# First modulation quarter copied by ScalarE and turned in another PSUM tag; at the end, last squares summed by TensorE and two products on GpSimd

## The chip, the cores and the metric

The kernel runs on one core of one Trainium2 chip. The metric is the device time of one execution in microseconds (us), from the start of the program to its end. The core's engines work in parallel, each through a list of instructions in its own fixed order, and wait for one another through semaphores: TensorE (PE; its weight loads are shown as PEld), VectorE (DVE), ScalarE (ACT), GpSimd (POOL) and SyncE (SP), which here only issues DMA transfers.

## The reference

The program is the trunk of a diffusion model: two layers over 512 latent and 256 context tokens, model width 1024, batch 1, in fp32, and a final RMSNorm of the latent tokens. Each layer scales and shifts its normalised input by a modulation vector that is computed from the conditioning vector (adaLN), runs two mixers in parallel on it, adds their output, and then runs an MLP with a hidden width of 4096:

```python
def rmsnorm(x, w):
    y = xf * lax.rsqrt(jnp.mean(xf * xf, axis=-1, keepdims=True) + NORM_EPS)
    return (y * w.astype(F32)).astype(x.dtype)
def modulate(h, shift, scale):
    return h * (1.0 + scale) + shift
def sq_relu_mlp(h, w1, w2):
    return jnp.square(jax.nn.relu(h @ w1)) @ w2
```

Layer 0 has global attention beside a bidirectional RWKV-7 scan, whose state carries from token to token: S_t = S_{t-1} (diag(w_t) - kk_t^T (a_t * kk_t)) + v_t^T k_t, y_t = S_t r_t. Layer 1 has windowed attention beside a bidirectional Mamba-2 mixer. The output is the latent stream after the last RMSNorm.

## The kernel before

Activations lie with the model width on the 128 partitions (eight tiles, k = 0 to 7) and tokens along the free axis. Every large product is made of three passes in fp32r: each operand is split in a rounded part and a remainder (`split`, L279 on ACT and L280 on DVE, tiles whi/wlo for weights, hh/hl or dh/dl for activations), and PE adds whi·hh, whi·hl and wlo·hh in PSUM (`product`, L367; the rows are named after what they make: win, wout, m). Weights come from memory in 512 KB pieces through SP into tiles wraw (and wmod for the modulation's), a few ahead.

The code says what depends on what; the order in which each engine's instructions stand is set by a scheduler that plays the whole program through with simulated times (`schedule_with_timeline_sim=True`) and takes what is ready, with parts of the code marked as urgent (`tc.high_priority()`). So an edit in one place can move instructions far from it. Tiles come from pools with a number of buffers; PSUM tiles go by tags ("s", "mod", "w"), and a tile waits until the one before it in its tag is free.

Three places matter.

*The head.* The first product of layer 0 (`win`) needs the modulation of layer 0 and the norm of x. `first_modulation(q)` makes one of four quarters: 4 times 16 matmuls (L428) into PSUM tile mod, a copy into SBUF (mrows, L431), a turn by PE (modt, L433), and an addition of the bias on DVE (modT, L435). For quarter q the tiles k = 2q and 2q+1 of the normed input follow: nscale (L452), ny (L497), hh (L498), hl (L500). The norm is made by squares (nsq, L470), their sums over k (acc, L471), `rms_rows`: sums over partitions by PE against ones (nsum, L479), a power -1/2 on DVE and POOL (nr, L381, L382), split (nrs), a diagonal (ndiag, L486), and a broadcast by PE (nbc, L490); ACT copies it for later use (rb, L550).

*Scan and attention of layer 0.* The scan goes through the tokens in steps (rows s, x, xs, u, vu, y, yacc by name) and leaves PE waiting between steps; the attention's matmuls (scores sc, turned probabilities pt, values po) fill in. The results go through memory (oD) and come back as the operand of the output product: `raw<-oD` (L1293), split into xr and dh/dl, then `wout` (L1302). yt turns the scan's output, gg are gates that are loaded for it (L1087, L1088), oy is the gated output.

*The tail.* The MLP of layer 1 does its last products (m, eight tiles) first for the first half of the latent tokens, LATS[0], then for the second, LATS[1]. Each tile is added to xl (`update`, L1223) and squared (`add_squares`; the last addition is on DVE). `to_out` scales xl by the norm's weight (L1768), calls `rms_rows`, and multiplies pairs of tiles by the broadcast row (L1778), and SP sends them out (L1779). For the first half the row is first copied to SBUF (rms, L1773). In the product the variable `eng` is set and not used:

```python
                eng = G if s == LATS[0] and k < 4 else V
                V.tensor_tensor(out=xs, in0=xs, in1=bc.unsqueeze(1).to_broadcast([P, 2, s[1]]), op=ALU.mult)
```

Of the kernel before, what the change touches and what calls it, by code (L numbers as in the profile page):

```python
# [18 lines left out]
P = 128  # L19
D = 1024  # L20
KT = 8
# [203 lines left out]
def tile_trunk(ctx: ExitStack, tc: tile.TileContext, t: dict, out, cc: Cols, pc: Cols):  # L225
# [69 lines left out]
    def at(t, s):  # L295

        if s == OUTER:
            return t[:, NCTX:NT].rearrange("p (b c) -> p b c", c=P)[:, ::3]
        return t[:, s[0]:s[0] + s[1]]
# [50 lines left out]
    def row(x, k, s):  # L350
        return x.at(k, s) if isinstance(x, Stream) else at(x[:, k], s)
# [67 lines left out]
    def first_modulation(q, np_):  # L419

        ps = psum("mod", "mod")
        for kp in range(KT // 2):
            wm = np_.tile([P, 1024], F32, tag="wm", name=u("wmod"), bufs=6)
            nc.sync.dma_start(wm, t["wmod0"][q, kp])
            for j in range(2):
                k = 2 * kp + j
                for r in range(4):
                    T.matmul(ps[32 * r:32 * r + 32, 0:P], lhsT=cs[:, k, :], rhs=wm[:, 512 * j + P * r:512 * j + P * r + P],  # L428
                             start=k == 0, stop=k == KT - 1, tile_position=(0, 32 * r))
        rows = np_.tile([P, P], F32, tag="mrows", name=u("mrows"), bufs=2)  # L430
        V.tensor_copy(out=rows, in_=ps[:, 0:P])  # L431
        pt = psum("s", "modt")
        T.transpose(pt[:, 0:P], rows, ident)  # L433
        ks = slice(2 * q, 2 * q + 2)
        V.tensor_tensor(out=modT[:, 0, 0:16, :].rearrange("p (s k) v -> p s k v", s=2)[:, :, ks],  # L435
                        in0=pt[:, 0:P].rearrange("p (s k r) -> p s k r", s=2, k=2)[:, :, :, 0:2],
                        in1=Q("bmod", 0, 16).rearrange("p (s k) -> p s k", s=2)[:, :, ks].unsqueeze(3).to_broadcast([P, 2, 2, 2]),
                        op=ALU.add)
# [22 lines left out]
    onesr = cp.tile([P, P], F32R, name="onesr")  # L461
    V.tensor_copy(out=onesr, in_=ones)

    def add_squares(np_, acc, x, k, s, eng=G):

        if k == 0:
            A.activation(out=at(acc, s), in_=row(x, k, s), func=AF.Square)
            return
        sq = np_.tile([P, NT], F32, tag="nsq", name=u("nsq"), bufs=2)
        A.activation(out=at(sq, s), in_=row(x, k, s), func=AF.Square)  # L470
        (V if k == KT - 1 else eng).tensor_tensor(out=at(acc, s), in0=at(acc, s), in1=at(sq, s), op=ALU.add)  # L471

    def rms_rows(np_, acc, s, tag):

        n = s[1] // P
        pr = psum(tag, "nsum")
        for i in range(n):
            c = s[0] + (P if s != OUTER else NLAT - P) * i
            T.matmul(pr[:, 2 * i:2 * i + 2], lhsT=acc[:, c:c + P], rhs=ones[:, 0:2], start=True, stop=True)  # L479
        r = np_.tile([P, 4], F32, tag="nr", name=u("nr"))[:, 0:n]  # L480
        rsqrt(r, pr[:, 0:2 * n:2], 1.0 / D, EPS, n)
        rr = [np_.tile([P, 4], F32R, tag=f"nr{j}", name=u("nrs"))[:, 0:n] for j in (0, 1)]
        split(rr[0], rr[1], r)
        dg = np_.tile([P, 2, n, P], F32R, tag=f"ndiag{n}", name=u("ndiag"))
        for j in (0, 1):
            V.tensor_tensor(out=dg[:, j], in0=ident.unsqueeze(1).to_broadcast([P, n, P]),  # L486
                            in1=rr[j].bitcast(F32).unsqueeze(2).to_broadcast([P, n, P]), op=ALU.mult)
        bc = psum(tag, "nbc")[:, 0:n * P]
        for j in (0, 1):
            T.matmul(bc, lhsT=onesr, rhs=dg[:, j], start=j == 0, stop=j == 1)  # L490
        return bc
# [733 lines left out]
    def mlp(mp, md, l, x, acc, segs, hh, hl, first, parts, then, side=iter(())):  # L1225
# [4 lines left out]
        for g in range(MLPG):  # L1230
# [14 lines left out]
            for n, part in enumerate(parts if last else (segs,)):  # L1245
                for q in range(4):
                    w = weight(t["w2"][l, g, q])
                    if g:
                        advance(side)
                    for i in range(2):  # L1250
                        m = 2 * q + i
                        ps = psum("w", "m2")
                        product([(ps, w, 512 * i)], dh, dl, range(4), (part,))
                        with tc.high_priority() if last and n == len(parts) - 1 else ExitStack():
                            update(l, 5, x, ps, m, part)
                            for s in part if last else ():
                                add_squares(mp, acc, x, m, s, V if n == len(parts) - 1 else G)
                with tc.high_priority() if last and n == len(parts) - 1 else ExitStack():
                    for s in part if last else ():
                        then(s)  # L1260
# [485 lines left out]
    with ExitStack() as se:  # L1746
# [18 lines left out]
        def to_out(s):  # L1765
# [9 lines left out]
            for k in range(0, KT, 2):  # L1775
                xs = xl[:, k:k + 2, ts]
                eng = G if s == LATS[0] and k < 4 else V
                V.tensor_tensor(out=xs, in0=xs, in1=bc.unsqueeze(1).to_broadcast([P, 2, s[1]]), op=ALU.mult)  # L1778
                nc.sync.dma_start(out[:, k:k + 2, ts], xs)  # L1779

        mlp(mp, md, 1, x, acc, LAT, hh, hl, LATS, [(s,) for s in LATS], to_out)
# [22 lines left out]
```

## Time and profile before

| | |
|---|---|
| time, three runs | 2007.57, 2012.63, 2013.88 us (median 2012.63) |
| profiled execution | 2009.51 us, its span 2007.7 us |
| mean granted clock of PE | 0.975 of full speed |
| busy | PE 94%, PEld 77%, DVE 61%, ACT 42%, POOL 15% of the span |
| DMA | 228.18 MB, 113 GB/s over the span |

The profile is of one execution. The span goes from its first instruction to its last. The chain is followed back from the last instruction to whatever released each one; its shares say which engine the end hung on. A row of a group gives the line, engine and operation, output and inputs with their shapes, how often, then busy time in all and the mean in ns of one, then the idle time just before and who ended it.

### The profile page before, as it was taken

How to read it: one execution, taken by the hardware profiler on the slowest of the kernel's cores; microseconds unless marked ns; L12 is line 12 of the kernel's file. 1: busy time of each engine (PE TensorE's matmuls, PEld its weight loads, DVE VectorE, ACT ScalarE, POOL GpSimd, SP SyncE). 2: the span in 40 equal slices, each digit the busy share in tenths (PEclk: the TensorE clock that was granted, in tenths of full speed). 3: DMA queues.
4: the chain of work that ended last, by engine and by line, in shares of the span. 5: the costliest groups of instructions: out<-in, count | busy, mean ns of one | idle time of the engine just before them, and what ended most of it. 6: DMA issues, size and time to landing. Idle time of an engine off the chain costs nothing.

```text
span 2007.7 us, 34218 instructions
## 1 busy us (share of the span) xinstructions
PE 1896.6 (94%) x13992; PEld 1545.1 (77%) x13992; DVE 1215.2 (61%) x2150; ACT 840.7 (42%) x1419; POOL 294.2 (15%) x291
## 2 busy tenths in 40 slices
PE   6999988899998999999999999899899789999997
PEld 4776756776765998888888889778578488888886
DVE  5567979775677765654544444865687464444445
ACT  3344442555544552232223224544566454333335
POOL 0000014432321520000000002310153120000001
PEclk9999998899998999999999999999999799999998
DMA  9355575742414733344444422212101133333333
GB/s 336 121 166 171 182 228 148 156 89 56 98 44 132 251 107 99 122 124 136 125 125 121 136 84 80 76 53 74 32 1 53 32 95 105 95 92 97 95 97 113
DMA packets 147884, 228.18 MB, mean 114 GB/s; under 512 B 65024, under 2 KB 102288, under 8 KB 147600
## 3 DMA queue, kind: packets, MB, share of 16 engines
q1 hardware_dynamic: 140912, 213.54, 36.1%
q10 hardware_dynamic: 5456, 7.73, 1.1%
q0 software_dynamic: 1360, 4.73, 0.7%
q8 instruction: 110, 1.80, 0.4%
q14 instruction: 46, 0.38, 0.1%
HBM read 200.00 MB, written 25.96 MB: 113 GB/s over the span
## 4 chain that ended last, share of the span: by engine, by line
PE 77%; DVE 9%; DMA 7%; ACT 3%; issue 3%; POOL 1%; SPq 0%; DVEq 0%; POOLq 0%; ACTq 0%
PE m L367 37%; PE win L367 13%; PE po L341 4%; DMA wmod<-in_wmod_dram 4%; PE pt L332 3%; PE z L985 2%; DVE wlo L280 2%; PE sc L1147 2%; PE wout L1718 1%; PE wout L1302 1%; PE s L1051 1%; PE mod L405 1%; PE lora L653 1%; PE z L1560 1%; DVE junk L1319 1%
## 5 line engine op out<-in xcount | busy, mean ns | idle before, releaser
L279 ACT ACTIVATE whi<-wraw 128x1024 fp32r<-128x1024 f32 x214 | 226.4, 1059 | 678.0 <-PE m L367 561.0
L280 DVE TENSOR_TENSOR wlo<-wraw,whi 128x1024 fp32r<-128x1024 f32 x214 | 264.4, 1236 | 212.2 <-ACT whi L279 209.4
L367 PE MATMUL m<-hh,whi 128*128 128x512 f32 (+1 forms) x816 | 239.3, 344 | 4.9 <-ACT relu L1241 2.4
L367 PE MATMUL m<-hl,whi 128*128 128x512 f32 (+1 forms) x816 | 241.2, 343 | 0.2 <-POOL hl L503 0.2
L367 PE MATMUL m<-hh,wlo 128*128 128x512 f32 (+1 forms) x816 | 241.3, 344 | 0.0
L367 PE MATMUL m<-dl,whi 128*128 128x256 f32 (+1 forms) x832 | 240.7, 341 | 0.0
L367 PE MATMUL m<-dh,whi 128*128 128x256 f32 (+1 forms) x832 | 238.6, 342 | 1.7 <-DVE xl L1223 1.6
L367 PE MATMUL m<-dh,wlo 128*128 128x256 f32 (+1 forms) x832 | 239.8, 341 | 0.1
L367 PEld LDWEIGHTS m<-dh,whi 128*128 128x128 f32 x832 | 153.3, 188 | 23.9 <-DVE xl L1223 4.9
L367 PEld LDWEIGHTS m<-hh,whi 128*128 128x128 f32 x816 | 152.1, 188 | 24.7 <-ACT relu L1241 2.8
L471 POOL TENSOR_TENSOR acc<-acc,nsq 128x256 f32<-128x256 f32 x42 | 42.8, 1027 | 865.8 <-ACT nsq L470 861.0
L367 PEld LDWEIGHTS m<-hl,whi 128*128 128x128 f32 x816 | 153.6, 188 | 19.4 <-POOL hl L503 0.4
L367 PEld LDWEIGHTS m<-dl,whi 128*128 128x128 f32 x832 | 153.8, 188 | 19.0
L367 PEld LDWEIGHTS m<-dh,wlo 128*128 128x128 f32 x832 | 153.7, 188 | 18.9 <-DVE wlo L280 0.3
L367 PEld LDWEIGHTS m<-hh,wlo 128*128 128x128 f32 x816 | 153.4, 188 | 19.0 <-DVE wlo L280 0.3
L367 PE MATMUL win<-hl,whi 128*128 128x512 f32 (+1 forms) x512 | 162.3, 348 | 4.7 <-POOL hl L503 3.5
L367 PE MATMUL win<-hh,whi 128*128 128x512 f32 (+1 forms) x512 | 162.3, 362 | 2.7 <-ACT hh L498 2.7
L367 PE MATMUL win<-hh,wlo 128*128 128x512 f32 (+1 forms) x512 | 160.2, 345 | 0.0
L1319 DVE SCALAR_TENSOR_TENSOR junk<-wmod,crow 128x1024 f32<-128x1024 f32 x64 | 78.5, 1226 | 118.5 <-DMA wmod<-in_wmod_dram 117.9
L1223 DVE SCALAR_TENSOR_TENSOR xl<-m,modT,xl 128x512 f32<-128x512 f32 (+1 forms) x144 | 97.4, 686 | 72.3 <-PE m L367 72.3
L367 PEld LDWEIGHTS win<-hh,whi 128*128 128x128 f32 x512 | 95.4, 194 | 33.6 <-issue 15.7
L367 PEld LDWEIGHTS win<-hl,whi 128*128 128x128 f32 x512 | 98.5, 193 | 22.9 <-issue 5.7
(413 smaller groups left out, 3560.0 us busy)
## 6 DMA issues: line engine op xcount, KB each, us to landing
wraw<-in_w_dram SPq DMA_DIRECT2D x136, 512.0 KB, 3.6
wmod<-in_wmod_dram SPq DMA_DIRECT2D x96, 512.0 KB, 4.2
wraw<-in_wout_dram SPq DMA_DIRECT2D x40, 512.0 KB, 3.7
wraw<-in_win_dram SPq DMA_DIRECT2D x35, 512.0 KB, 4.4
arD<-ar SPq DMA_DIRECT2D x8, 768.0 KB, 4.5
kbD<-kb SPq DMA_DIRECT2D x8, 768.0 KB, 6.5
ari<-arD SPq DMA_DIRECT2D x24, 256.0 KB, 3.9
kbd<-kbD SPq DMA_DIRECT2D x48, 128.0 KB, 3.9
```

The costliest lines, as they stand in the source:

```text
L279: A.activation(out=hi, in_=src, func=AF.Copy)
L280: (lo_eng or V).tensor_tensor(out=lo, in0=src, in1=hi.bitcast(F32), op=ALU.subtract)
L332: T.transpose(pt[:, P * j:P * j + P], prob[j][:, P * m:P * m + P], ident)
L341: T.matmul(po[HALVES[i], :], lhsT=vt[:, k_, r], rhs=w_, start=m_ < 2, stop=m_ + 2 >= n, tile_position=(0, 64 * i))
L367: T.matmul(part(ps, s), lhsT=a[:, c], rhs=row(b, k, s), start=first and j == 0 and q == 0, stop=last and j == n - 1 and q == 2)
L405: T.matmul(ps[r:r + 32, :], lhsT=cs[:, k, :], rhs=wm[:, c], start=k == 0, stop=k == KT - 1, tile_position=(0, r))
L471: (V if k == KT - 1 else eng).tensor_tensor(out=at(acc, s), in0=at(acc, s), in1=at(sq, s), op=ALU.add)
L653: T.matmul(ps[s][d][:, 0:s[1]], lhsT=LORA[wname][r, P * p:P * p + P], rhs=src[r, tokens(s)], start=True, stop=True, tile_position=(64 * d, 0))
L985: T.matmul(ps[:, P * (2 * a + c):P * (2 * a + c) + P], lhsT=kb[:, 2 * m + a, c, :], rhs=ar[:, 2 * m + a, c, :], start=True, stop=True)
L1147: T.matmul(ps[:, cols2(s)], lhsT=qs[:, 2 * j + g, :], rhs=kx[:, g, s[0]:s[0] + s[1]], start=m == 0, stop=m == 1)
L1223: V.scalar_tensor_tensor(out=xs, in0=part(ps, s), scalar=mod(l, which, m, s[2]), in1=xs, op0=ALU.mult, op1=ALU.add)
L1319: V.scalar_tensor_tensor(out=junk, in0=wm, scalar=1.0, in1=crow[:, :, v], op0=ALU.mult, op1=ALU.mult, accum_out=modT[:, l, n, v:v + 1])
```

## The change

It makes three edits. In `first_modulation` the copy of PSUM to mrows goes from DVE to ACT, for all four quarters, and the turn of the first quarter takes a PSUM tile of tag "mod" and not "s". In the MLP of layer 1 the last square (m = 7) of the second half of the latent tokens is not added to acc but kept (`held`), and `rms_rows` adds it by a second matmul into the same PSUM columns. In `to_out` the variable `eng` takes effect: for the first half, the products of tiles 0, 1 and 2, 3 are made by GpSimd.

```diff
-        V.tensor_copy(out=rows, in_=ps[:, 0:P])
-        pt = psum("s", "modt")
+        A.activation(out=rows, in_=ps[:, 0:P], func=AF.Copy)
+
+        pt = psum("s" if q else "mod", "modt")
...
+    held = {}
+
-    def add_squares(np_, acc, x, k, s, eng=G):
+    def add_squares(np_, acc, x, k, s, eng=G, hold=False):
...
         A.activation(out=at(sq, s), in_=row(x, k, s), func=AF.Square)
+        if hold:
+            held[s] = sq
+            return
         (V if k == KT - 1 else eng).tensor_tensor(out=at(acc, s), in0=at(acc, s), in1=at(sq, s), op=ALU.add)
...
-            T.matmul(pr[:, 2 * i:2 * i + 2], lhsT=acc[:, c:c + P], rhs=ones[:, 0:2], start=True, stop=True)
+            terms = [acc] + ([held[s]] if s in held else [])
+            for j, v in enumerate(terms):
+                T.matmul(pr[:, 2 * i:2 * i + 2], lhsT=v[:, c:c + P], rhs=ones[:, 0:2], start=j == 0, stop=j == len(terms) - 1)
+        held.pop(s, None)
...
-                                add_squares(mp, acc, x, m, s, V if n == len(parts) - 1 else G)
+                                add_squares(mp, acc, x, m, s, V if n == len(parts) - 1 else G, l == 1 and n == len(parts) - 1 and m == KT - 1)
...
-                V.tensor_tensor(out=xs, in0=xs, in1=bc.unsqueeze(1).to_broadcast([P, 2, s[1]]), op=ALU.mult)
+                eng.tensor_tensor(out=xs, in0=xs, in1=bc.unsqueeze(1).to_broadcast([P, 2, s[1]]), op=ALU.mult)
```

The order of instructions moves in the head, in the stage of scan and attention, and in the tail. The lines of the changed kernel are up to nine higher than those of the one before.

PE in the head, before, from the last group of the first quarter's matmuls (mod_215) on; mod_338 is the second quarter:

```order
L428 MATMUL mod_215<-wmod_246,cs 32x128 x7
L490 MATMUL nbc_210<-ndiag_207,onesr 128x512 [waits DVE_49] x2
L428 MATMUL mod_338<-wmod_339,cs 32x128 [waits DMAHW1_49,DVE_49]
L428 MATMUL mod_338<-wmod_339,cs 32x128 x7
L433 MATMUL modt_258<-cst,mrows_256 128x128 [waits Activation_49]
L428 MATMUL mod_338<-wmod_349,cs 32x128 [waits DMAHW2_49]
```

The same place in the changed kernel:

```order
L428 MATMUL mod_215<-wmod_246,cs 32x128 x7
L499 MATMUL nbc_210<-ndiag_207,onesr 128x512 [waits DVE_49]
L434 MATMUL modt_258<-cst,mrows_256 128x128 [waits Activation_49]
L499 MATMUL nbc_210<-ndiag_207,onesr 128x512 [waits DVE_49]
L428 MATMUL mod_338<-wmod_339,cs 32x128 [waits DMAHW1_49,DVE_49]
L428 MATMUL mod_338<-wmod_339,cs 32x128 x7
L428 MATMUL mod_338<-wmod_349,cs 32x128 [waits DMAHW2_49]
```

The turn modt stands between the two broadcasts now, ahead of both groups of the second quarter.

PE at the end of the scan, before: the last y, then the first row of the output product (wout):

```order
L1072 MATMUL y_7041<-vu_7039,z_3287 64x64
L1116 MATMUL yt_7072<-cst,yacc 128x128 [waits DVE_49,PE_49]
L1116 MATMUL yt_7072<-cst,yacc 128x128 x3
L1147 MATMUL sc_5701<-kh,qs_5245 128x256 [waits Activation_49]
L1147 MATMUL sc_5701<-kl,qs_5245 128x256
L1147 MATMUL sc_5701<-kh,qs_5245 128x512
L1147 MATMUL sc_5701<-kl,qs_5245 128x512
L332 MATMUL pt_5725<-cst,prob_5688 128x128 [waits Activation_49]
L332 MATMUL pt_5743<-cst,prob_5688 128x128
L1302 MATMUL wout_7184<-xr,whi_7180 128x256 [waits PE_49,Activation_49]
```

And in the changed kernel, where all of sc and pt stands further up:

```order
L341 MATMUL po_5724<-pts_5871,vtok 64x512 [waits Activation_49]
L1079 MATMUL y_7041<-state_6986,ard_3282 64x64
L1081 MATMUL y_7041<-vu_7037,z_3286 64x64
L1081 MATMUL y_7041<-vu_7039,z_3287 64x64
L341 MATMUL po_5724<-pts_5887,vtok 64x512 [waits DVE_49]
L1311 MATMUL wout_7184<-xr,whi_7180 128x256 [waits Activation_49]
```

The attention's last values (po), which stood behind the first wout before, now stand in front of it, and the scores and turns that stood between y and wout are gone from there. On SP, in the same place, both pairs of gg now stand ahead of raw<-oD; before, a half of raw came first and the second pair came later.

PE in the tail, before and then in the changed kernel: the broadcast row of the first half, the sums of the second half, its broadcast row:

```order
L490 MATMUL nbc_18453<-ndiag_18450,onesr 128x256 [waits DVE_49,PE_49]
L490 MATMUL nbc_18453<-ndiag_18450,onesr 128x256 [waits DVE_49]
L479 MATMUL nsum_18632<-cst,acc_15666 128x2 [waits DVE_49]
L479 MATMUL nsum_18632<-cst,acc_15666 128x2
L490 MATMUL nbc_18645<-ndiag_18642,onesr 128x256 [waits DVE_49,PE_49]
```
```order
L499 MATMUL nbc_18453<-ndiag_18450,onesr 128x256 [waits DVE_49]
L487 MATMUL nsum_18631<-cst,acc_15666 128x2 [waits DVE_49]
L487 MATMUL nsum_18631<-cst,nsq_18621 128x2 [waits Activation_49]
L487 MATMUL nsum_18631<-cst,acc_15666 128x2
L487 MATMUL nsum_18631<-cst,nsq_18621 128x2
L499 MATMUL nbc_18646<-ndiag_18643,onesr 128x256 [waits DVE_49,PE_49]
```

The sums wait for ACT's last square itself (nsq_18621) and no longer for its addition on DVE. On POOL the two products of the first half stand in a row ahead of the power (L382) of the second half; on DVE the last acc and two of the four products of the first half are gone from ahead of nr.

## Prediction

> **What bounds the kernel now.** I read the page first: busy times, the 40 slices and the chain that ended last.
>
> ```profile
> PE 1896.6 (94%) x13992; PEld 1545.1 (77%) x13992; DVE 1215.2 (61%) x2150; ACT 840.7 (42%) x1419; POOL 294.2 (15%) x291
> PE   6999988899998999999999999899899789999997
> ...
> PE 77%; DVE 9%; DMA 7%; ACT 3%; issue 3%; POOL 1%; SPq 0%; DVEq 0%; POOLq 0%; ACTq 0%
> ```
>
> TensorE (PE) is the bound: 1896.6 of 2007.7 us, and 77% of the chain. No part of the change takes a product away (it adds two small matmuls), so it can only win or lose PE's idle time, 111 us in all, and clock lost to cold restarts. The lowest slices are the first (6), one near 1580 us and the last (7 each); the change names the first and the last. Because a scheduler orders all instructions by its own simulated times, I compared the order of before and after everywhere. It moved in three places: the head (0 to 72 us), the stage in which the recurrent scan and the attention of layer 0 share PE (310 to 650 us), and the tail. Between them a shift made early is carried on, since PE is the bound there.
>
> **Head.** The timeline of its critical stretch (start, duration, engine; in brackets the idle time before, and who ended it):
>
> ```profile
> 24.73 1.08 PE L428 MATMUL mod<-wmod,cs 128*32 128x128 f32 x16 [1.98 <-DMA wmod<-in_wmod_dram]
> ...
> 25.95 1.28 DVE L486 TENSOR_TENSOR ndiag<-cst,nrs 128x512 fp32r<-128x512 f32 x2
> ...
> 26.69 1.40 PE L490 MATMUL nbc<-ndiag,onesr 128*128 128x512 f32 x2 [0.88 <-DVE ndiag L486]
> 27.16 0.28 DVE L431 COPY mrows<-mod 128x128 f32<-128x128 f32 x1
> ...
> 28.12 0.60 ACT L550 ACTIVATE rb<-nbc 128x512 f32<-128x512 f32 x1 [3.24 <-PE nbc L490]
> ...
> 29.02 0.47 PE L433 MATMUL modt<-cst,mrows 128*128 128x128 f32 x1
> 29.43 1.08 PE L428 MATMUL mod<-wmod,cs 128*32 128x128 f32 x16
> ...
> 30.52 0.51 ACT L498 ACTIVATE hh<-ny,modT 128x256 fp32r<-128x256 f32 x1 [0.86 <-DVE ny L497]
> ...
> 31.08 2.52 PE L367 MATMUL win<-hh,whi 128*128 128x256 f32 x6 [0.57 <-ACT hh L498]
> ...
> 43.09 0.62 PE L367 MATMUL win<-hh,whi 128*128 128x256 f32 x3 [0.50 <-ACT hh L498]
> ```
>
> The first quarter's sums are ready at 25.81, but DVE copies them only at 27.16, behind ndiag, and the turn (modt) stands behind a whole modulation group until 29.02. ACT stands idle from 24.9 to 28.1, so a copy by ACT starts near 25.85. Its duration is not in the trace; the nearest row is DVE's 0.28 for the same tile, and ACT's 0.60 for four times as much bounds it from above. So mrows is there by 26.4 at the latest. The new order of PE puts modt between the two nbc: nbc 26.69 to 27.4, modt to 27.9 (0.47 each way as before), nbc to 28.6. The second nbc is 0.5 later, and with it rb: 28.6 to 29.2 on ACT. The chain after modt (modT, nscale, ny, hh) took 31.03 - 29.49 = 1.54, so hh could be there at 29.8. But now PE's two mod groups at 1.08 stand ahead of the first product: 28.6 + 2.16 = 30.8. PE starts win at 30.7 to 30.8 instead of 31.08: -0.3. PE, not hh, is then the gate, and this is the most that this gap (0.57) can return. The second gap, 0.50 at 43.09, waits for the second quarter; the new order has win products in front of it, so it may vanish: -0.5. What ACT takes over are three more copies of 0.3 to 0.6, ahead of hh pieces that PE needs; ACT's load hides them:
>
> ```profile
> 31.00:72.00 41.00, 40.41 (x336) 28.78 (x336) 24.45 (x51) 13.76 (x24) 0.58 (x5) 1.00 0.65 237
> ```
>
> (stretch, then busy PE, PEld, DVE, ACT, POOL, the clock, DMA share, GB/s). ACT is busy for 13.76 of 41 and PE idle for only 0.6 of it, so little more than the gaps is to be had by waits. SP now issues one load of weights (wraw) behind one of modulation (wmod): at the row's 237 GB/s its 512 KB come 2.2 us later. It is used only behind the fourth quarter, and the DMA engines are free for a third of the stretch: nothing. What remains is clock. The six matmuls of 128x256 at 31.08 took 2.52 (0.42 each), the three at 43.09 took 0.62 (0.21 each): win's first 3.1 us ran at half speed and lost 1.55. If the gap's closing lets the clock rise before win, this comes back. The trace speaks for it only so far: PE was busy from 26.69 to 30.5 without the clock rising, with small gaps in it. I take the head at -1.5, between -0.8 and -0.8 - 1.55 = -2.35; the lower bound of the gain is 0, if an ACT copy lands ahead of an hh that PE waits for. The Trainium skill (TensorE: Matmul & The Clock Gate, Part 1) says that about 3.4 us of sustained work open the clock, in a window that runs freely; the 3.1 us agree with its length, and by it the head would be -2.35 or -0.8 by the window's phase.
>
> **Scan and attention, 310 to 650 us.** Nothing of the diff is in it; only the order of instructions moved. Windows, with the same columns, then the chain across its end, and PE's rows there:
>
> ```profile
> 310.00:400.00 90.00, 78.61 (x879) 65.31 (x880) 75.98 (x195) 37.45 (x87) 38.93 (x26) 0.91 0.68 165
> 400.00:500.00 100.00, 96.82 (x1440) 72.06 (x1439) 68.72 (x161) 55.02 (x109) 30.98 (x29) 0.97 0.33 72
> 500.00:600.00 100.00, 98.83 (x1381) 70.72 (x1379) 71.45 (x159) 53.45 (x98) 28.27 (x25) 1.00 0.32 74
> 600.00:626.00 26.00, 25.40 (x360) 16.72 (x356) 17.09 (x40) 12.30 (x23) 1.86 (x2) 1.00 0.06 16
> ```
> ```profile
> 624.74 0.36 SPq L1087
> 625.15 0.50 SPq L1088
> 625.75 5.73 DMA raw<-oD
> ...
> 633.97 2.93 PE wout L1302 x12
> ...
> 639.15 1.00 PE po L341 x2
> ...
> 648.54 7.14 PE wout L1302 x59
> ```
> ```profile
> 623.95 0.33 PE L1072 MATMUL y<-vu,z 128*64 128x64 f32 x3
> ...
> 626.71 0.44 PE L332 MATMUL pt<-cst,prob 128*128 128x128 f32 x2 [0.86 <-ACT prob L1156]
> 632.71 0.58 PE L1302 MATMUL wout<-xr,whi 128*128 128x256 f32 x1 [5.55 <-ACT xr L279]
> 633.97 0.58 PE L1302 MATMUL wout<-xr,whi 128*128 128x256 f32 x1 [0.68 <-DVE xr L280]
> ```
>
> Work is fixed here, so the stage's end shifts by the change in PE's idle time: 11.4 + 3.2 + 1.2 + 0.6 = 16.4 before 626, and 0.86 + 5.55 + 0.68 = 7.1 from there to 633.97. That wait is the scan's output going to memory and back (raw<-oD, 5.73). Before, yt, sc and pt stood between the last y (to 624.3) and 626.7, and six pairs of po were left for after the wait (639.15 to 648.54, 9.4 us). In the new order all po come before the first wout, and yt after 29 of its matmuls: from the last y to wout only one po is left. The gap before wout is then, po at half of a pair's 1.00, 633.97 - 624.3 - 0.5 = 9.2 instead of 7.1: +2.1. On SP both pairs of gg now go before raw, and the second pair waits for the last oy of the group before; the loads before raw's second half take 0.36 + 0.50 longer: +0.5 (0 to +0.9). Against it, the 8 us of attention moved ahead may fill some of the 16.4 idle: the 11.4 lie where DVE is busy for 75.98 of 90, and 5.0 in the rest. I take -1.6 (0 to -6). Sum +1, from -4 to +3, and up to +6 if the scan's own chain, with its steps in a new order, waits more.
>
> **Tail.** DVE, then ACT, then PE and POOL in the last microseconds:
>
> ```profile
> 1994.28 0.41 DVE L471 TENSOR_TENSOR acc<-acc,nsq 128x256 f32<-128x256 f32 x1
> 1994.61 2.49 DVE L1778 TENSOR_TENSOR xl<-xl,rms 128x512 f32<-128x512 f32 x4
> 1997.01 0.42 DVE L471 TENSOR_TENSOR acc<-acc,nsq 128x256 f32<-128x256 f32 x1
> ```
> ```profile
> 1994.11 0.38 ACT L1773 ACTIVATE rms<-nbc 128x256 f32<-128x256 f32 x1 [0.17 <-PE nbc L490]
> 1994.39 0.42 ACT L470 ACTIVATE nsq<-xl 128x256 f32<-128x256 f32 x1
> ```
> ```profile
> 1997.49 1.02 PE L479 MATMUL nsum<-cst,acc 128*128 128x2 f32 x4 [3.42 <-DVE acc L471]
> ```
> ```profile
> 1998.84 0.70 POOL L382 TENSOR_TENSOR nr<-nr,mhalf 128x2 f32<-128x2 f32 x1 [9.70 <-DVE nr L381]
> ```
>
> The last square is ready at 1994.81, yet its addition waits on DVE behind four products until 1997.01. After: DVE's acc of the square before it ends at 1994.69, the held square goes straight to PE, and nsum starts at 1994.87 instead of 1997.49, 2.6 earlier. It has eight matmuls for four: 1.02 more at this pace, half of it if the clock is still up; so the sums are there by 1995.9 to 1996.9 (before 1998.51). DVE does two products for four, 1994.69 to 1995.95. Then the power on POOL, at 1998.84 before, now queues behind POOL's two products. Their price is not in the trace; the nearest rows:
>
> ```profile
> L1017 POOL TENSOR_TENSOR old<-state,dds 128x512 f32<-128x512 f32 x22 | 24.4, 1110 | 96.2 <-DVE state L1059 94.0 <-DVE st L1155 2.0
> ...
> L471 POOL TENSOR_TENSOR acc<-acc,nsq 128x256 f32<-128x256 f32 x42 | 42.8, 1027 | 865.8 <-ACT nsq L470 861.0 <-issue 4.2
> ```
>
> At L1017's 1.11 each, from 1994.5 (rms ready), they end at 1996.8 with a small gap, the power starts 2.0 earlier. If DVE's two (0.62 each) and POOL's two take turns, 3.46, they end at 1998.0: 0.8 earlier. At 2.1 each (twice L1017) the power starts where it did: 0. The trace shows that they disturb each other:
>
> ```profile
> 1980.27 1.73 DVE L280 TENSOR_TENSOR wlo<-wraw,whi 128x1024 fp32r<-128x1024 f32 x1 [0.37 <-ACT whi L279]
> ```
> ```profile
> 1981.08 1.52 POOL L471 TENSOR_TENSOR acc<-acc,nsq 128x256 f32<-128x256 f32 x1 [0.16 <-ACT nsq L470]
> ```
> ```profile
> L280 DVE TENSOR_TENSOR wlo<-wraw,whi 128x1024 fp32r<-128x1024 f32 x214 | 264.4, 1236 | 212.2 <-ACT whi L279 209.4
> ```
>
> while POOL ran acc, against 1.24 on average (264.4 us over 214). I take -1 (0 to -2), near the turns. The Trainium skill (SBUF — State Buffer, Who interferes with whom) has a DVE instruction with two SBUF inputs and a GpSimd one that reads SBUF block each other for their whole length; by it the tail would be -0.8, which this row bears out only in part, since 1.73 is less than 1.24 + 1.52. From the power on, the rows are as before: nrs, ndiag, nbc, four products, the output.
>
> **Sum.** -1.5 + 1 - 1 = -1.5. The profiled execution took 2009.51 us (span 2007.7), so one like it would take 2008.0. It stands 3.1 below the median of the runs shown, 2012.63; those run from 2007.57 to 2013.88, and with the profiled one their mean is 2010.9. I forecast that mean less 1.5: 2009.4.
>
> **Rivals.** (1) Slower: the reordered scan exposes its own chain. A scan step passes PE, DVE, ACT and back, and only attention filler keeps PE at 97 to 99% in 400 to 600; in 310 to 400, where filler is short, PE idles for 11.4 of 90. Were filler used up so that another 90 us ran like that, it would cost 11 on top of the +2.1: with head and tail at -2.5, 2010.9 + 10.6 = 2021.5. It decides from +10 in the stage, a tenth off PE's busy share in one of the windows of 100 us. Against it: the same products are there to fill with, and only six po pairs moved. 12 in 100. (2) Faster: attention moved ahead fills the scan's idle time, -4 for the stage in place of +1, and with it come the head's -2.35 (clock up early) and the tail's -2: -8.4, 2002.5. It decides from -4.3 in all, as -1.8 in the stage with head and tail as forecast. For it: idle 16.4 before 626 is larger than the work moved. Against it: most of that idle lies in DVE's bound stretch. 24 in 100. (3) The tail's edit is eaten by its own queue, the power behind two slow POOL products: tail 0, the sum -0.5, 2010.4; within the forecast's own band, 20 of its 64 in 100. (4) The head's edit does nothing, ACT's copy only trading places with DVE's: 2010.9, also within.
>
> **How the numbers follow.** 0.3% of 2012.63 is 6.0 us, about what a measurement of this kernel can tell from no change, since three runs spread over 6.3. Forecast with (3) and (4), 2004.5 to 2014.5, 64 in 100, a twelfth of it (5) under 2006.6. Of (2)'s 24, 21 lie under it; of (1)'s 12, 11 over 2018.7. So faster by more than 0.3%: 0.26; slower: 0.11; same: 0.63. The range: 2001 for (2) with its low runs, 2017.5 for +6 in the middle with nothing won at head and tail (2016.9) and a little scatter; half of (1) and a third of (2) lie outside, about 15 in 100.
>
> **What would show it.** Right: modt near 27.4 and the first win near 30.8 without an idle bracket; nsum x8 near 1994.9 and one POOL row of two products ahead of the power; a bare gap of 8 to 10 before wout, then wout without po between. Wrong: PE busy under 95 in 400:500, a first win later than 31.1, or a power later than 1998.8 less the shift.

## The result, and the profile after

The changed kernel takes 2021.1 us (median of seven runs, 2016.98 to 2022.93). The kernel before, timed beside it, took 2005.12 to 2013.88 in six runs (median 2010.1). So the changed one takes 1.0054 times as long, with a 95% interval of 1.0039 to 1.007. It is slower, and the forecast of 2009.4 (range to 2017.5) was wrong. Medians and ratios (of the means), here and below, leave out two slow runs, one of the kernel before (2352.13) and one of e11 (4954.29). The profiled execution took 2022.93 us, its span 2021.2, which is 13.5 more than the span before. The page's busy times, slices and chain shares:

```profile
PE 1895.9 (94%) x13996; PEld 1546.3 (77%) x13996; DVE 1212.7 (60%) x2143; ACT 842.2 (42%) x1423; POOL 298.3 (15%) x293
PE   6999988899997999999999999899899799999997
...
PE 74%; DVE 11%; DMA 7%; ACT 4%; issue 3%; POOL 1%; SPq 0%; DVEq 0%; POOLq 0%; ACTq 0%
```

PE was busy as long as before (1895.9 for 1896.6), so the 13.5 us are idle time of PE. The chain says where they went, from PE's share (77 to 74%) to DVE's (9 to 11%).

**Head.** The same stretch as before, ACT's copy first, then PE, and the window to the end of the block:

```profile
25.90 0.28 ACT L431 ACTIVATE mrows<-mod 128x128 f32<-128x128 f32 x1 [1.00 <-PE mod L428]
```
```profile
26.51 0.79 PE L499 MATMUL nbc<-ndiag,onesr 128*128 128x512 f32 x1 [0.68 <-DVE ndiag L495]
27.11 0.41 PE L434 MATMUL modt<-cst,mrows 128*128 128x128 f32 x1
27.17 0.78 PE L499 MATMUL nbc<-ndiag,onesr 128*128 128x512 f32 x1
27.88 1.94 PE L428 MATMUL mod<-wmod,cs 128*32 128x128 f32 x32
29.74 0.80 PE L367 MATMUL win<-hh,whi 128*128 128x256 f32 x2
...
30.98 0.41 PE L367 MATMUL win<-hh,wlo 128*128 128x256 f32 x1
...
31.39 0.28 PE L367 MATMUL win<-hl,whi 128*128 128x256 f32 x1
...
40.95 0.62 PE L367 MATMUL win<-hh,whi 128*128 128x256 f32 x3 [0.71 <-ACT hh L507]
```
```profile
31.00:72.00 41.00, 39.67 (x339) 27.86 (x339) 21.99 (x46) 13.59 (x26) 0.58 (x5) 1.00 0.70 250
```

The edit does here what it says: the copy at 25.90, modt at 27.11, the first win at 29.74 without a bracket (before 31.08), and a product of 256 columns falls from 0.41 to 0.28 near 31.2, where before the clock rose at 34.2. But the gap for the second quarter stayed (0.71 at 40.95, before 0.50), and the long run of win at the block's end starts, by the chain that ended last from 60 to 95 us, only 0.93 earlier. Before, then after:

```profile
71.49 16.92 PE win L367 x96
```
```profile
70.56 16.93 PE win L367 x96
```

**Scan and attention.** First two of the windows that stand in the prediction, now of the changed kernel. A window between fixed times mixes work that has shifted, so the stage is then cut at its own milestones, for the kernel before and then for the changed one. The cuts are the first qksum (a sum of squares for the norm of the attention's queries and keys, ahead of the scan), the scan's first and last state update on DVE, the first wout, and 130 us beyond that:

```profile
400.00:500.00 100.00, 97.06 (x1484) 71.42 (x1484) 71.28 (x166) 58.83 (x117) 34.47 (x30) 1.00 0.35 76
500.00:600.00 100.00, 94.74 (x1298) 66.84 (x1297) 64.58 (x140) 49.94 (x91) 27.10 (x25) 0.98 0.31 75
```
```profile
313.14:376.57 63.43, 55.44 (x451) 46.62 (x452) 57.22 (x142) 18.78 (x40) 27.09 (x15) 0.87 0.73 182
376.57:613.47 236.90, 232.20 (x3463) 171.41 (x3462) 165.07 (x383) 131.73 (x259) 70.49 (x63) 0.99 0.33 74
613.47:632.71 19.24, 12.46 (x145) 6.98 (x143) 13.74 (x31) 7.31 (x12) 2.27 (x3) 0.88 0.42 132
632.71:762.71 130.00, 126.00 (x943) 116.52 (x944) 88.40 (x134) 66.82 (x103) 46.02 (x41) 0.98 0.55 173
```
```profile
313.80:383.38 69.58, 58.48 (x454) 49.11 (x454) 54.89 (x146) 20.92 (x46) 24.97 (x15) 0.80 0.73 177
383.38:632.36 248.98, 237.68 (x3488) 171.64 (x3487) 169.69 (x386) 136.40 (x264) 72.77 (x63) 0.99 0.30 70
632.36:651.75 19.39, 10.52 (x144) 6.51 (x143) 13.17 (x28) 4.70 (x7) 3.99 (x4) 0.85 0.66 208
651.75:781.75 130.00, 124.41 (x945) 119.58 (x946) 88.01 (x134) 63.96 (x97) 44.61 (x40) 0.97 0.51 159
```

A stretch's length less PE's busy time is PE's idle time: 8.0, 4.7, 6.8 and 4.0 us before, 11.1, 11.3, 8.9 and 5.6 after. The stretches are called A, B, C and D below. The sum goes from 23.5 to 36.9, +13.4; the time from the first qksum to the last update of xl (the addition of the MLP's last tile, where the tail begins) goes from 1680.73 to 1694.07, +13.3. So the whole loss is idle time of PE in this stage, and half of it lies in B, the scan's middle.

How far one trace can be trusted is shown by the experiments below, of which three leave this stage in the order before (e3, e4, e9) and one has the changed kernel's (e1). In the four traces with the order before, A idles 7.3 to 9.0 us and D 4.0 to 5.7, but B 4.7 and C 6.8 in every one; e1 has 11.3 in B and 9.1 in C. So what B and C lose belongs to the order, and D's 5.6 is within the scatter. From the first qksum to the last update of xl the four traces take 1680.7 to 1685.4 us and the two 1694.1 and 1695.1: by the means 12.0 more, where the single pair gave 13.3. In C the wait for the scan's result is as forecast; the chain and PE's rows:

```profile
643.87 6.59 DMA raw<-oD
...
653.01 4.73 PE wout L1311 x27
```
```profile
642.55 0.28 PE L1081 MATMUL y<-vu,z 128*64 128x64 f32 x2
651.75 0.80 PE L1311 MATMUL wout<-xr,whi 128*128 128x256 f32 x2 [8.87 <-ACT xr L279]
653.01 0.58 PE L1311 MATMUL wout<-xr,whi 128*128 128x256 f32 x1 [0.47 <-DVE xr L280]
```

The bare gap is 8.87 + 0.47 = 9.3 (forecast 9.2). In B no wait is large. The greatest waits of PE there, after and then before (time in all, count, longest):

```profile
PE sc L1156 <- ACT prob L1163: 2.7, 6, 1.2
PE xv L1011 <- DVE zk L1000: 2.5, 2, 1.5
PE u L1045 <- DVE xs L1038: 1.5, 3, 0.9
```
```profile
PE z L985 <- ACT z L994: 2.3, 1, 2.3
PE sc L1147 <- ACT prob L1154: 1.0, 2, 0.8
```

They belong to the attention's own chain (sc waits for prob), to the preparation of later scan steps (xv) and to the step itself (u): many waits of a microsecond, none of which carries the 6.6 by itself. Added up by the engine that PE waited for, over all rows of this view, they show a pattern: before, 4.3 us for ACT and 0.3 for DVE (the same in e3, e4 and e9); after, 4.8 for ACT and 6.3 for DVE (4.7 and 6.3 in e1). So B's loss, by the releasers that the profile infers, is PE's waits for DVE, of which xv has 3.5, u 1.5, y 0.7 and s 0.6. DVE is busy for 169.69 of B's 248.98 us, so it is not its load as a whole. Its instructions come in another order, and why that order makes PE wait was not traced further.

**Tail.** DVE, then POOL, in the last microseconds:

```profile
2007.87 0.48 DVE L1232 SCALAR_TENSOR_TENSOR xl<-m,modT,xl 128x256 f32<-128x256 f32 x1 [0.60 <-PE m L367]
...
2008.61 3.45 DVE L1787 TENSOR_TENSOR xl<-xl,rms 128x512 f32<-128x512 f32 x2
2011.98 0.14 DVE L381 TENSOR_SCALAR nr<-nsum 128x2 f32<-128x2 f32 x1
```
```profile
2008.57 2.94 POOL L1787 TENSOR_TENSOR xl<-xl,rms 128x512 f32<-128x512 f32 x2 [5.43 <-ACT rms L1782]
2012.27 0.70 POOL L382 TENSOR_TENSOR nr<-nr,mhalf 128x2 f32<-128x2 f32 x1 [0.76 <-DVE nr L381]
```

From the start of the last update of xl to the end of the program it is 13.33 us, before 13.83.

### The profile page after: what moved, and what is told of

The parts are those of the page before. It is cut to its first block, busy times and chain, and to the rows that moved or that the text cites. A ratio compares the mean times of both kernels' runs of the same rounds, so it can differ in the third digit from the quotient of the medians.

```text
span 2021.2 us, 34230 instructions
## 1 busy us (share of the span) xinstructions
PE 1895.9 (94%) x13996; PEld 1546.3 (77%) x13996; DVE 1212.7 (60%) x2143; ACT 842.2 (42%) x1423; POOL 298.3 (15%) x293
## 4 chain that ended last, share of the span: by engine, by line
PE 74%; DVE 11%; DMA 7%; ACT 4%; issue 3%; POOL 1%; SPq 0%; DVEq 0%; POOLq 0%; ACTq 0%
PE m L367 37%; PE win L367 12%; DMA wmod<-in_wmod_dram 4%; PE po L341 4%; PE pt L332 2%; PE wout L1311 2%; DVE wlo L280 2%; PE z L994 2%; PE wout L1727 1%; PE sc L1156 1%; PE lora L662 1%; PE s L1060 1%; DVE junk L1328 1%; PE z L1569 1%; PE mod L405 1%
## 5 line engine op out<-in xcount | busy, mean ns | idle before, releaser
L367 PEld LDWEIGHTS win<-hh,whi 128*128 128x128 f32 x512 | 95.7, 194 | 34.2 <-issue 14.7
```

The costliest lines, as they stand in the source:

```text
L367: T.matmul(part(ps, s), lhsT=a[:, c], rhs=row(b, k, s), start=first and j == 0 and q == 0, stop=last and j == n - 1 and q == 2)
```

## The experiments

Two theories on the loss stood against each other, and both take it to come from the re-ordered stage, which the head's edit sets off. The first: the attention that filled PE's idle time is used up too soon, since it stands earlier in the new order. The rival: the scan's own chain is held up at its start, where DVE's first vu (its result in the scan's first step) stands behind the attention's casts (qs, the attention's queries, rounded and split for PE). Twelve kernels, e1 to e12, each have part of the edit or something added. All ratios are to the kernel before on the same chip, whose medians were 2009.86 (first four), 2010.36 (next four) and 2008.62 (last four).

**Which edit.** e1_head has the edit in `first_modulation` alone, e3_tail the two edits of the tail alone, e4_held the held squares alone:

```diff
 e4_held, against the changed kernel
-        A.activation(out=rows, in_=ps[:, 0:P], func=AF.Copy)
-        pt = psum("s" if q else "mod", "modt")
+        V.tensor_copy(out=rows, in_=ps[:, 0:P])
+        pt = psum("s", "modt")
...
-                eng.tensor_tensor(out=xs, ...)
+                V.tensor_tensor(out=xs, ...)
```

> The edit in first_modulation alone, tail as before. Theory A (the copy by ACT shifts the scheduler's simulated times, and that reorders scan and attention of layer 0): its order between 310 and 650 us is the changed kernel's row for row, so the first wout starts near 652 (before 634) and the time is that of the changed kernel plus the 0.5 us that its tail gains: ratio to before 1.0055, +10 to +14 us. Theory B (the tail's products on GpSimd cost the time): same as before or up to 1 us faster, 0.9995 to 1.000. Theory C (ACT's extra copies cost time at the head): the loss shows ahead of 310 us.

> The held squares and the two products on GpSimd, head as before. Order up to the tail is that of before. Theory A: time within 1 us of before (ratio 0.999 to 1.001), the last update of xl to the end shorter by 0.5 us as in the changed kernel. Theory B: slower by 8 us or more.

> Only the held squares; all four products of the first half stay on DVE. Theory L (DVE's and GpSimd's products shut each other out of SBUF, so that moving two to GpSimd gave nothing): DVE does four in 2.5 us, nr starts 0.7 to 0.8 earlier after the last update of xl than in the changed kernel (3.3 instead of 4.1 us), the tail is 13.8 - 1.3 = 12.5 us long. Theory M (products on GpSimd run beside DVE's, the tail is bound elsewhere): the same 13.3 as in the changed kernel, or longer.

Measured: e1 2022.39 us, 1.0056 (1.0044 to 1.0068), all of the loss; e3 2009.0, 1.0 (0.9988 to 1.0012), nothing. In e1 the instructions of the stage stand in the changed kernel's order on every engine; in e3 and e4 they stand as before. The PE idle times of A to D are 39.5 us in e1, 24.5 in e3, 26.0 in e4. e4 was run once (2010.38); its tail, read from the trace, is 12.33 us long against 13.25 in e3:

```profile
1997.00 2.49 DVE L1786 TENSOR_TENSOR xl<-xl,rms 128x512 f32<-128x512 f32 x4
1999.41 0.15 DVE L381 TENSOR_SCALAR nr<-nsum 128x2 f32<-128x2 f32 x1
```

DVE alone makes all four products in 2.49 and is then free for nr; with two of them on GpSimd, DVE's own two take 3.45. So the held square is worth about -1.5 (from 13.83) and the two products on GpSimd cost 0.9 to 1.0 of it. Other traces agree: the tail is 12.27 to 12.35 us long in the three kernels with the held square alone (e4, e9, e11), 13.25 to 13.33 in those with the products on GpSimd as well, and 13.46 to 13.92 in those with the tail of before.

**Which line of the head's edit.** e7_tag changes only the first quarter's PSUM tag. e10_q0 moves only the first quarter's copy to ACT. e9_q12_held moves only the second and third quarters' copies, with the held square:

```diff
 e9_q12_held (e10_q0: q in (0,); e7_tag: V.tensor_copy for all, and the tag of the change)
+        if q in (1, 2):
+            A.activation(out=rows, in_=ps[:, 0:P], func=AF.Copy)
+        else:
+            V.tensor_copy(out=rows, in_=ps[:, 0:P])
+        pt = psum("s", "modt")
```

> Only the PSUM tag of the first quarter's turn is changed (copies stay on DVE, tail as before). The order of scan and attention comes out differently again, and again no po is left behind the first wout; DVE's first vu stands behind two qs. Theory R (any shift of the scheduler's simulated times rolls a new order of this stage, and the order before was a lucky one): slower by 3 to 14 us, ratio 1.002 to 1.007, although one PSUM tag is all that was edited. Theory E (it is ACT's copy that hurts): 0.999 to 1.001.

> Only the copy of the first quarter goes to ACT, all else as before. The row is taken from DVE at the head and put on ACT; 300 us later the order of scan and attention comes out new, no po is left behind wout, and DVE's first vu stands behind one of the two first qs. Theory R: slower by 5 to 12 us through that stage, ratio 1.0025 to 1.006. Theory H (a copy at the head can only matter at the head): 0.999 to 1.0005.

> ACT copies only quarters 1 and 2 of the modulation (0 and 3 stay on DVE, all turns in tag s as before), the last squares held, no product on GpSimd. The scheduler leaves every other row in its place, so nothing rolls: theory R gives the time of before less 1.5 us of tail and up to 0.5 at the head, ratio 0.9985 to 1.0005. If ACT's copies cost time by themselves: 1.001 or more.

Measured: e10 2017.92, 1.0041 (1.0027 to 1.0055), slower; e7 2014.84, 1.0024 (1.0013 to 1.0036), a little slower; e9 2006.84, 0.9996 (0.9985 to 1.0007), the same. In e9 all rows of the stage stand as before; e7 and e10 each give the stage an order of its own. So two of ACT's copies, where they leave the order as it is, cost nothing measurable. One copy of 0.28 us on another engine, or a PSUM tag, 290 us ahead of the scan, gives the stage another order. That it does so by way of the scheduler's simulated times fits how the scheduler is built; no run shows those times. In e10's scan (B) PE idles for 245.86 - 233.66 = 12.2 us, in the changed kernel's for 11.3. Its stretches A and B:

```profile
314.56:379.81 65.25, 57.08 (x460) 48.53 (x461) 59.03 (x149) 21.04 (x47) 23.55 (x15) 0.86 0.79 184
379.81:625.67 245.86, 233.66 (x3486) 171.13 (x3484) 169.89 (x387) 136.22 (x263) 72.77 (x63) 0.99 0.31 72
```

e7 moves something else as well. Before and e7, from 72 us to the first qksum, and PE's wait for the modulation's weights in that stretch:

```profile
72.00:313.14 241.14, 226.53 (x1869) 163.45 (x1867) 176.95 (x318) 95.98 (x157) 29.27 (x30) 0.96 0.54 170
```
```profile
72.00:303.40 231.40, 221.45 (x1858) 160.07 (x1857) 176.07 (x318) 94.67 (x155) 27.79 (x30) 1.00 0.57 176
```
```profile
PE mod L405 <- DMA wmod<-in_wmod_dram: 6.0, 3, 3.1
```
```profile
PE mod L405 <- DMA wmod<-in_wmod_dram: 0.7, 2, 0.5
```

Its first qksum comes at 303.40. In the four traces with the order before it comes at 308.3 to 313.1, by their mean 7 us later. Part of that is idle time (14.6 us before, 10.0 in e7) and part the clock, which was at 0.96 in this trace of before and 1.00 in e7's. e7 then loses more than it won: 37.2 us idle in A to D.

**Is the filler used up?** e2_late is the changed kernel with its last block of attention pushed back, by a lower priority for the scheduler, so that some of it is left for the wait before wout; e8_before_late does the same to the kernel before:

```diff
+        def later(gen):
+            ...
+                with tc.high_priority(-800):
+                    ...
+                        next(gen)
+                    ...
-        attention = steps(*fill)
+        attention = steps(*fill[:-1], *[later(g) for g in fill[-1:]])
```

> All three edits, but the last attention block of layer 0 gets a lower priority by 800 program steps, so that six pairs of po stand behind the first wout again, as before the change. Theory A1 (what costs the time is that the attention is used up before the scan's output comes back from memory, so that both trips of raw<-oD are bare): the gap after wout's first waits is filled again and at least 10 of the 14.9 us that the middle lost come back: ratio 0.9985 to 1.001. Theory A2 (the new interleaving inside the scan costs the time, whatever is left for the end): only the 2 to 5 us at the end come back, ratio 1.003 to 1.0045, and PE between 345 and 640 stays as idle as in the changed kernel.

> The kernel before, only the last attention block at lower priority by 800: the order up to about 560 us stays, and two more pairs of po and pt go behind the first wout. Theory W (attention that is left fills the two waits for raw<-oD): same or up to 3 us faster, ratio 0.9985 to 1.000. Theory V (what is put behind wout only delays wout): slower by 1 to 5 us.

Measured: e2 2023.33, 1.006 (1.0045 to 1.0075), no better than the change and above what either theory allowed; e8 2012.21, 1.0013 (1.0003 to 1.0023). In e2 the six po pairs stand behind the first wout again, and C is short, but the idle time came back in D:

```profile
625.86:639.23 13.37, 6.53 (x125) 5.08 (x119) 12.27 (x29) 5.15 (x8) 2.46 (x3) 0.87 0.52 166
639.23:769.23 130.00, 121.30 (x912) 111.43 (x913) 87.39 (x133) 66.01 (x103) 44.45 (x40) 0.97 0.55 172
```

130.00 - 121.30 = 8.7 us, where the changed kernel has 5.6 and the one before 4.0. The theory of the used-up filler falls, as far as it concerns the wait before wout: giving filler back to the wait gave no time back, and the kernel before, with its filler pushed back, idles 28.4 us instead of 23.5.

**Is the scan held up at its start?** DVE's rows at the first vu, before and then after:

```profile
363.93 0.88 DVE L1041 SCALAR_TENSOR_TENSOR vu<-u,cst,vm 128x256 f32<-128x256 f32 x2 [0.43 <-PE u L1036]
364.83 1.22 DVE L1137 TENSOR_TENSOR qs<-qr,qs 64x1024 fp32r<-64x1024 f32 x1
```
```profile
364.97 1.22 DVE L1146 TENSOR_TENSOR qs<-qr,qs 64x1024 fp32r<-64x1024 f32 x1 [3.11 <-ACT qs L1145]
...
367.84 1.22 DVE L1146 TENSOR_TENSOR qs<-qr,qs 64x1024 fp32r<-64x1024 f32 x1 [1.64 <-ACT qs L1145]
369.09 0.88 DVE L1050 SCALAR_TENSOR_TENSOR vu<-u,cst,vm 128x256 f32<-128x256 f32 x2
```

Before, vu goes ahead of the casts. After, it stands behind two of them, and each waits for ACT's copy of qr: counted from the first qksum, the first vu comes at 55.3 us instead of 50.8 (50.0 to 51.3 in the four traces). e5_gate makes the first two blocks' casts wait for the scan's first vu, by one element that is written from it (a gate). So that vu exists by then, it also takes out the loop that puts 40 steps of attention ahead of the scan in the code. e6_gate_late adds the late block, and e12_before_gate puts the same gate into the kernel before, where vu stood ahead of the casts already:

```diff
+            if first:
+                V.tensor_copy(out=qs[0:1, 0, 0:1], in_=first[0][0:1, 0, 0:1])
...
             A.activation(out=qs, in_=qr, func=AF.Copy)
...
+                    if b == 0 and j == 0:
+                        first.append(vu[0])
...
-        for _ in range(40):
-            advance(attention)
```

> All three edits, and the casts of the first two attention blocks' queries (qs) must wait for the scan's first vu by a tiny extra copy on DVE, so that DVE's and ACT's first scan rows no longer stand behind casts that wait for a load (qr). In the traces the stretch from the first qksum near 310 us to the first state update took 63.4 to 63.8 us in the two kernels without the edit of the head and 69.6 to 70.2 in the three with it. Theory S (the scan's start waits for qr): that stretch is 63 to 65 us here, 5 to 6 us come back, ratio 1.002 to 1.004. Theory N (that stretch is long for another reason): 68 to 70 us and the ratio stays at 1.005 to 1.006.

> As the one before, and the last attention block at lower priority by 800 as well. If the loss is the sum of a late start (6 us), waits inside the scan (6 to 7 us of idle PE) and a bare wait at its end (2 to 4 us), this one keeps only the second: ratio 1.001 to 1.004. If start and end are all, 0.999 to 1.001. If nothing but the interleaving in the scan counts, 1.005.

> The kernel before with that wait of qs for the first vu, which stood in that order anyway. Its order from there on is a new one. Theory R: the start of the scan stays at 63 to 65 us, and the rest of the stage is longer than before by 2 to 9 us: ratio 1.001 to 1.0045. If the order inside the scan does not matter: 0.999 to 1.0005.

Measured: e5 2018.47, 1.0041 (1.0028 to 1.0055); e6 2013.5, 1.0019 (1.0008 to 1.0031); e12 2018.05, 1.0043 (1.0029 to 1.0057). e5's stage up to the scan's last state, and its first vu on DVE:

```profile
309.60:376.16 66.56, 54.89 (x456) 45.98 (x458) 55.42 (x146) 20.30 (x44) 25.34 (x15) 0.90 0.76 183
376.16:621.01 244.85, 241.35 (x3504) 173.46 (x3502) 166.77 (x389) 136.75 (x262) 68.63 (x63) 0.99 0.32 70
```
```profile
360.68 0.88 DVE L1050 SCALAR_TENSOR_TENSOR vu<-u,cst,vm 128x256 f32<-128x256 f32 x2 [2.89 <-PE u L1045]
```

The vu is back at 360.68 - 309.60 = 51.1 us, and A lost 3.0 of its 6.2 us, between what the two theories expected. But A's idle time stayed (11.7). B's fell to 3.5, in a stretch only 4 us shorter. e6 shows no gain in A at all (69.44), and e12, where nothing was to be mended, lost 0.43%. Against the means of the four traces with the order before, e12's trace is 5.4 us longer from the first qksum to the last update of xl, 3.3 of it as idle time in A to D, for a timed loss of 8.6 to 9.4; where the rest lies stays open. The clearest answer is in e10, which has no gate: its first vu comes at 52.0 us, its A is 65.25 us long (62.6 to 65.1 in the four traces) and idles no longer than theirs, and it still loses 0.41%. So the hold-up can be seen in the rows, but most of the loss comes without it, and the gate is itself a new order. e11_tag_gate_held joins e7's tag (copies on DVE), the gate and the held square:

> The tag of the first quarter's turn changed, the first casts of qs behind the first vu, and the last squares held. The tag's order won some 7 us ahead of 310 us in its run and lost 11 behind it; if the late start (6 us) is what the extra wait mends, the sum is -7 + 5 - 1.5: ratio 0.9975 to 0.9995, faster than both. If the order that comes out waits elsewhere: 1.000 to 1.003.

Measured: 2008.1 (median), 0.9999 (0.9988 to 1.0009), the same as before, at the edge of what was expected if the new order waits elsewhere. Its first qksum comes at 303.61, some 7 us early as in e7, and the tail brings 1.5. The stage takes most of that back: 1688.9 us from the first qksum to the last update of xl, 30.4 of A to D idle.

**All orders side by side.** PE's idle time in A to D, what of it lies in B, and the timed ratio:

| order of the stage | idle, us | in B, us | ratio |
|---|---|---|---|
| as before: before, e3, e4, e9 | 23.5, 24.5, 26.0, 24.5 | 4.7 in each | 1, 1.0, one run, 0.9996 |
| e12 | 27.9 | 4.1 | 1.0043 |
| e6 | 28.2 | 3.8 | 1.0019 |
| e8 | 28.4 | 5.8 | 1.0013 |
| e5 | 30.4 | 3.5 | 1.0041 |
| e11 (7 us won ahead of the stage) | 30.4 | 3.9 | 0.9999 |
| e10 | 35.3 | 12.2 | 1.0041 |
| e2 | 36.7 | 8.4 | 1.006 |
| changed kernel (e1: the same order, 39.5, 1.0056) | 36.9 | 11.3 | 1.0054 |
| e7 (7 us won ahead of the stage) | 37.2 | 11.5 | 1.0024 |

Ten orders in all, and in these traces each of the nine other than that before idles longer. For e12, e6 and e8 the step from 26.0 (1.9 to 2.4 us) is no larger than the scatter of one order (2.5), and their timed ratios are the better evidence. Idle time isn't the whole of it either: from the first qksum to the last update of xl, PE is also busy for 1619.8 to 1620.7 us in e2, e5, e6 and e12, above the 1613.6 to 1618.2 of the order before. That the loss is the new order's, set off by the head's edit, is shown by e1, e3, e7, e9 and e10; e8 and e12, with new orders and the old head, lose too. Why the order before is the best of these is shown only in pieces: the wait before wout (+2.1) and PE's waits for DVE in B (+6.0). What DVE does ahead of each of them, and what the first vu costs, stays open. No version beats the kernel before beyond its interval; e9_q12_held, equal to it, is faster than the changed kernel.

## Why the prediction was wrong, point by point

- *The step that failed* is the sum for scan and attention: "Sum +1, from -4 to +3, and up to +6 if the scan's own chain, with its steps in a new order, waits more." Measured: +13.3 in this pair of traces, +12.0 by the means of four and two. With the head's -0.9 and the tail's -0.5, +12.0 makes +10.6, and the timed 0.54% is 10.9. The idle time before the last state was to fall by 1.6, since attention moved ahead would fill it. It grew, by 3.1 in A and 6.6 in B, where PE's waits for DVE went from 0.3 to 6.3. The order of PE at the stage's end was read closely and priced rightly (+2.1 forecast; idle in C went from 6.8 to 8.9, and the bare gap measured 9.3 against 9.2). The further +0.5 for the loads ahead of raw did not show in it, though raw itself grew from 5.73 to 6.59. The 300 us ahead of it were priced by what moved in total, as though a stage with the same work idles about the same. e7, e10, e2 and e5, with 30.4 us of idle time and more, show that it does not.
- *Rival (1)*, slower by an exposed scan at 2021.5, came true in place, sign and size (2021.1), at 12 in 100. Its reason, filler used up, did not: e2 and e8 speak against it. That its size came so near is luck. What it had against it, "the same products are there to fill with", was true and did not help. Its sign on the page did not come: no window of 100 us lost a tenth of PE's busy share. PE was busy for 94.74 in 500:600 (before 98.83), and for 97.06 in 400:500, where "under 95" was named.
- *Head*, -1.5 forecast, -0.9 measured in one pair of traces (that long run of win starts at 70.1 to 71.3 in five traces with the whole edit of the head). The first win came earlier than the 30.7 to 30.8 forecast (29.74), since the second nbc followed modt at once and the 32 mod matmuls took 1.94, not 2.16. The clock rose 3 us earlier too. What failed was the -0.5 for the second gap. The chain that ended last, from 28 to 60 us, passes there through DVE's wlo and only then modT, on which the second quarter's hh hangs:

```profile
38.34 1.23 DVE wlo L280
39.56 0.09 DVE modT L436
```

  PE's own turn ended hardly sooner, at 39.44 (started 39.11, 0.33 long), so its place in PE's order counts as much as wlo. PE idled 41.00 - 39.67 = 1.3 of the window, 0.7 more than before. Of that, 0.5 is a wait of the fourth quarter's turn for ACT's copy (at 51.84), which the window of before doesn't have. The 0.9 can't be seen in the timed runs: the first qksum, at 313.80 for 313.14, comes at times that spread by 5 us in traces of one order (last section).
- *SP's reordered load in the head* was costed at nothing; ACT's one wait for wraw in the window grew from 1.4 to 2.0 us, and PE's chain does not pass through it.
- *Tail*, -1 forecast, -0.5 measured. The turns were right: forecast 3.46 for the four products, measured 2012.06 - 2008.57 = 3.49. By turns the forecast was -0.8, and I had taken -1. The rest is DVE's nr, which stands behind DVE's second product: the forecast let the power wait for POOL's two products alone. Rival (3), the tail eaten by its own queue, was two thirds right in size (1.0 of 1.5) and not in its way: POOL stood idle for 0.76 before the power, which waited for nr and so for DVE's slowed products, not for POOL's own.

## What to carry to other kernels

Where a scheduler orders everything by simulated times, an edit can be two changes: what it does, and the new order that it may deal to a tightly filled stage behind it. The second can be far larger (here -0.9 us at the head and +12 to +13 in the stage). Compare the orders first, line of the edit by line, and keep the lines that leave the rest in place (the copies of the second and third quarters, the held square). When a stage with 5% idle time is dealt anew, price it by how other orders of it came out, and not by the instructions that moved; here none of nine new orders idled less than the one before. And before work is given to GpSimd beside DVE, ask whether DVE alone is done sooner.

## What the runs showed of the hardware

DVE and GpSimd took turns on products with both inputs in SBUF: two and two took 3.49 us, four on DVE alone 2.49. The Trainium skill (SBUF — State Buffer, Who interferes with whom) says that such a pair block each other for whole instructions; this trace agrees, to 0.03 us of the sum by turns (3.46, from 0.62 and 1.11 for one). In the prediction I had held that rule to be borne out only in part.

PE's clock rose near 31.2 us, 4.7 us after PE's last idle gap (0.68, ended at 26.51). The Trainium skill (TensorE: Matmul & The Clock Gate, Part 1) has a free-running window of about 3.4 us that must be busy; by it the rise comes 3.4 to 6.8 us after the gap, an estimate from that page, and 4.7 lies in it. In the trace before, the rise near 34.2 came 3.1 us after the last gap (0.57, ended at 31.08), which is below that estimate. So one of the two traces agrees, and no run here shows how long a gap must be to count.

The first qksum came at 308.3 to 313.1 us in the four profiled executions (before, e3, e4, e9) whose order up to there is the same, but for the engine of two copies in e9. e1 and the changed kernel, with one order too, differ by as much (308.9 and 313.8). So a single trace can't show a gain under some 5 us in the first 310, and the stage had to be measured from its own start.
